# Encoder layer with window and neighbourhood attention: other times for the loads of keys and of the first gate, other places for buffers

## The chip, the cores and the metric

The kernel runs on one core of a Trainium2 chip. The metric is the device time of one execution in microseconds; "before" is the median of three runs. The engines are TensorE (PE in the profile, with its weight loads as PEld), VectorE (DVE), ScalarE (ACT), GpSimd (POOL) and SyncE (SP), which issues most DMAs. "SPq" is SP as a queue of DMA issues: it takes them strictly one after the other, and an issue that has to wait holds up all behind it.

## The reference

One layer of an encoder on 2048 tokens of width 1024, all in float32:

```python
z = rms_norm(x, norm_mix) @ w_in       # q_A k_A v_A q_B k_B v_B gate_A gate_B
yA = windowed_gqa(q_A, k_A, v_A, sink) # |t-s| <= 128, ALiBi, 8 heads, 2 of keys, one sink logit a head
yB = neighborhood_attn(q_B, k_B, v_B, rpb)  # 32 x 64 token grid, 8 x 16 neighbourhood, learned bias, 8 heads
x  = x + (sigmoid(gate_A) * (yA @ w_proj_a) + sigmoid(gate_B) * (yB @ w_proj_b)) @ w_out
x  = x + relu(rms_norm(x, norm_mlp) @ w_up) ** 2 @ w_down
out = rms_norm(x, norm_final)
```

## The kernel before, in words

Every large product is a sum of three matmuls (a high and a low part of each operand, lines 202 to 204 and 281 to 283), with float32 results in PSUM. The phases follow each other: norm and `w_in`, attention A, attention B, the end of the projections with `w_out`, up, down. Matrix work of another kind is put between the small matmuls of both attentions, so that PE has something to do while a softmax runs: in A the gates (`gate_tiles`), in B the last gates and then the projection of A's result (`proj_tiles`). `paced` deals this work out over the attention's units.

**Attention A** has 32 units. Its score is written by L858 and L859, its weights are turned by L893 and multiplied with the values by L878 and L879. L860 takes a unit's scores out of PSUM and adds a bias from `biasa0` or `biasa1`, one for each group of heads; the last units use `biasa1`. **Attention B** has 8 heads of 4 units (units 0 to 31, `attn_b`). A unit loads its queries (`qb`, L1094) and values (`vb`, L1097, a list `v_loads` keeps these loads), multiplies queries with the head's keys `kb` (L1107, four scores `s` of two matmuls), takes the scores out with a bias table added (L1112), exponentiates (L1118), scales them on GpSimd (L1123), turns the weights (L1153), splits them into `phb` and `plb` (L1159, L1160) and multiplies by the values (L1133). Keys of a head are 2 MB, in three DMAs (`load_k`, L1084 to L1086): the 128 rows, and the two halves of 64 rows with their places exchanged. Buffers `kb0` and `kb1` alternate with the head, so a head's load can start when the scores of the head before last are done. Bias tables (`biass` short, `biasl` long) are made by GpSimd (`make_bias_b`, L1075) from a raw table `braw` (L1061, L1063) and a mask.

**The projection** takes pairs of output columns f, f+1 for f = 0, 2, 4, 6. For each it loads and splits weights, and then for four pairs of (token blocks, column) loads a gate `z` of two halves (L996, 256 KB each), multiplies pages of y (`ypages`, the tiles `zh`) by the weights into the one PSUM buffer `mm`, and multiplies `mm` by the gate in place (L1013), which frees `mm`. The result goes out (`zp`, L175). One `z` is loaded ahead of the one in use.

**What sets the order.** The code emits instructions unit by unit, and a scheduler puts each engine's instructions into a row by its own estimates of when each can run; `tc.issue_after(x)` asks that a load be put behind instruction x. Pools are opened as two stacks in SBUF, from the left and from the right. Where B's pools lie on memory of A's, B's first load or write waits for A's last use of it. In before, `kb0` lies on `biasa1` and `ka0`, and so the keys of head 0 wait for the last unit of A to have used its bias.

Of the kernel before, what the change touches and what calls it, by code (L numbers as in the profile page):

```python
# [8 lines left out]
F32 = mybir.dt.float32  # L9
# [10 lines left out]
BH = 8  # L20
FF = 4096
EPS = 1e-6
P = 128
KC = D // P
NB = 4
BT = 512
# [23 lines left out]
def bias_layout():  # L50

    off, at = {}, 0
    start = []
    for j in (0, 1, 3):
        start.append(at)
        for i in (0, 1, 3):
            off[(JT[j], IT[i])] = at - start[-1]
            at += B_NR[i] * B_W[j]
        start.append(at)
    return off, start, at  # L60
# [32 lines left out]
def encoder_layer(ctx, tc, x, norm_mix, w_in, b_gate, sink, rpb, w_pa, w_pb, w_out,  # L93
                  norm_mlp, w_up, w_down, norm_final, dist_a, mask_b, out):
    nc = tc.nc
    V, A, G, PE, SY = nc.vector, nc.scalar, nc.gpsimd, nc.tensor, nc.sync

    def pool(name, side=None, space=None, stack=None):
        kw = {"reuse_waits": "tile"} if space is not DRAM else {}
        if side:  # L100
            kw["side"] = side
        if space:
            kw["space"] = space
        return (stack or ctx).enter_context(tc.tile_pool(name=name, bufs=1, **kw))

    def pools(stack, side, tags, name):

        return {t: pool(f"{name}_{t}", side=side, stack=stack) for t in tags}
# [9 lines left out]
    def psum(tag, bufs):  # L118
        n_ps[0] += 1
        return pps[tag].tile([P, 512], F32, tag=tag, bufs=bufs, name=f"{tag}_{n_ps[0]}")  # L120
# [3 lines left out]
    def T(pl, shape, dt, tag, bufs):  # L124
        n_t[0] += 1
        pl = pl[tag] if isinstance(pl, dict) else pl
        return pl.tile(shape, dt, tag=tag, bufs=bufs, name=f"{tag}_{n_t[0]}")
# [30 lines left out]
    zg = [[dp.tile([D, BT], F32, name=f"zg{b}{n}") for n in range(2)] for b in range(NB)]  # L158
# [11 lines left out]
    def put(dst, src):  # L170
        pending.append((dst, src))
# [5 lines left out]
    def split_weights(raw, hl, eng):  # L177
        A.copy(hl[:, 0], raw)
        eng.tensor_tensor(out=hl[:, 1], in0=raw, in1=hl[:, 0].bitcast(F32), op=ALU.subtract)
# [5 lines left out]
    def load_slice(parts):  # L185
        raw = T(wp, [P, KC, P], F32, "raw", 3)
        at = 0
        for ap, n in parts:
            SY.dma_start(raw[:, at : at + n, :], ap.rearrange("(k p) f -> p k f", p=P))
            at += n  # L190
        return raw

    def split_slice(raw, eng=G):
        hl = T(wp, [P, 2, KC, P], F32R, "whl", 2)
        split_weights(raw, hl, eng)
        return hl

    def cols(w, c, n=P):
        return w[:, c : c + n]

    def mm3(ps, lh, ll, rh, rl, first, last):
        PE.matmul(ps, lh, rh, start=first, stop=False)  # L202
        PE.matmul(ps, lh, rl, start=False, stop=False)  # L203
        PE.matmul(ps, ll, rh, start=False, stop=last)  # L204
# [373 lines left out]
    right = {n: (in_page[n](), in_page[n]()) for n in (1, 2)}  # L578
    tbanks = [(tpool, 2), (zpool[0], 1), (tpool, 2), (zpool[1], 1), (ypool[0], 1), (ypool[1], 1)]
    for k in range(KC):  # L580
        ps = zbank(*tbanks[k % 6])
        turned(ps, tiles[0], k)
        h, l = (t[:, k % 4] for t in right[1 + k // 4])
# [19 lines left out]
    for p in range(2):  # L603
        t = T(xp, [P, D], F32, "xin", 8).rearrange("p (k c) -> p k c", k=4)
# [15 lines left out]
    for k in range(KC):  # L620
# [8 lines left out]
        else:  # L629
            h, l = (t[:, kk] for t in right[3])  # L630
# [126 lines left out]
    for q in range(2, len(QUADS)):  # L757
# [5 lines left out]
        elif q in (6, 7):  # L763
            k = 2 * (q - 6)
# [8 lines left out]
        if q == SECOND:  # L773
            right, b0 = right2, 2
# [32 lines left out]
    wp = pools(s_w, "right", ("raw", "whl", "z"), "w")  # L807
    s_y = ExitStack()
    yb = T(pool("yb", side="left", stack=s_y), [P, BT], F32, "yb", 1)
    s_a = ExitStack()  # L810
    ap_ = pools(s_a, "left", ("dist", "sta", "qa", "ka1", "va1", "ya", "sa", "ph", "pl"), "a")
    ap_.update(pools(s_a, "right", ("biasa0", "va0", "ka0", "biasa1"), "a"))

    dist = T(ap_, [P, 384], F32, "dist", 1)
    SY.dma_start(dist, dist_a)
# [9 lines left out]
    ya = T(ap_, [P, BT], F32, "ya", 1)  # L825
# [158 lines left out]

    casts, now, v_loads = [], [0], []

    def proj_tiles(f):
        yield
        hl = split_slice(load_slice([(cols(w_pa[0], (f + i) * P), 4) for i in range(2)]), V)
        yield  # L990
        def load_z(b, i):
            z = T(wp, [P, 2, BT], F32, "z", 4)
            u = now[0] // 4 + 2
            with tc.issue_after(v_loads[u]) if u < len(v_loads) else nullcontext():
                for j in range(2):
                    SY.dma_start(z[:, j], zg[b + j][0][(f + i) * P : (f + i + 1) * P, :])  # L996
            return z

        z_next = load_z(0, 0)
        for b in (0, 2):  # L1000
            for i in range(2):
                z = z_next
                if b + i < 3:
                    z_next = load_z(*((b, 1) if i == 0 else (2, 0)))
                for j in range(2):
                    hi, lo = ypages[b + j]
                    ps = psum("mm", 1) if f + b < 8 else psum("s", 3)
                    for c in range(4):
                        cc = 4 * i + c
                        mm3(ps, hl[:, 0, cc, :], hl[:, 1, cc, :], hi[:, c], lo[:, c], c == 0, c == 3)  # L1010
                        if c == 1:
                            yield
                    V.scalar_tensor_tensor(out=z[:, j], in0=z[:, j], scalar=1.0, in1=ps, op0=ALU.add, op1=ALU.mult)  # L1013
                    put(zp[b + j][f + i], z[:, j])
                    yield

    fill = [gate_tiles(f) for f in range(14)] + [gate_tiles(14, 15)] + [proj_tiles(f) for f in range(0, 8, 2)]
    for n in (0, 0, 1):
        next(fill[n])
# [20 lines left out]


    s_b = ExitStack()
    bp = pools(s_b, "right", ("masks", "qb", "braw0", "biass", "stb", "kb0", "biasl", "braw1", "kb1"), "b")
    bp.update(pools(s_b, "left", ("sb0", "sb1", "vb0", "vb1", "sb2", "vb2", "phb", "plb"), "b"))
    boff, bstart, btotal = bias_layout()
    n_raw = [0]
    masks = T(bp, [P, btotal], mybir.dt.bfloat16, "masks", 1)
    with tc.issue_after(began[20]):
        SY.dma_start(masks, mask_b)
# [2 lines left out]
    def load_raw(h, jt):  # L1052
        j = (0, 1, 3)[jt]
        w = B_W[j]
        raw = T(bp, [P, 512], F32, f"braw{(n_raw[0] + 1) % 2 if n_raw[0] > 1 else 0}", 1)[:, : 16 * w]
        n_raw[0] += 1
        first = h * T_ROWS * w + (T_RO - 11) * w + (B_C0[j] - 16 * j - 15 + T_COFF[j])
        src = bass.AP(tabs[jt].tensor, tabs[jt].offset + first, [[w, 8], [1, 16], [1, 16 * w]])
        if n_raw[0] < 3:
            with tc.issue_after(began[20]):  # L1060
                SY.dma_start(raw, src)  # L1061
        else:
            G.dma_start(raw, src)  # L1063
        return raw

    def make_bias_b(raw, jt):
        j = (0, 1, 3)[jt]
        w = B_W[j]
        t = T(bp, [P, 40 * w], F32, "biasl" if jt == 1 else "biass", 1 if jt == 1 else 2)
        for i in (0, 1, 3):  # L1070
            n = B_NR[i] * w
            o = boff[(jt, IT[i])]
            at = (B_R0[i] - 8 * i + 4) * w
            out, mask, rows = t[:, o : o + n], masks[:, jstart[jt] + o : jstart[jt] + o + n], raw[:, at : at + n]
            G.tensor_tensor(out=out.rearrange("p (q x r) -> p q x r", x=w, r=4),  # L1075
                            in0=rows.rearrange("p (q r x) -> p q x r", x=w, r=4),
                            in1=mask.rearrange("p (q x r) -> p q x r", x=w, r=4), op=ALU.add)
        return t

    def load_k(h):  # L1080

        k = T(bp, [P, 2, S], F32R, f"kb{h % 2}", 1)
        kd = ks_b[h // 2][h % 2]
        SY.dma_start(k[:, 0].bitcast(F32), kd)  # L1084
        SY.dma_start(k[0:64, 1].bitcast(F32), kd[64:128])
        SY.dma_start(k[64:128, 1].bitcast(F32), kd[0:64])  # L1086
        return k

    def attn_b(n_u, h, j, k, bias):
        e, t = h % 2, h // 2  # L1090
# [74 lines left out]
    def all_b():  # L1165
        order = [(h, j) for h in range(BH) for j in ((0, 3, 1, 2) if h == 0 else range(4))]
        tables = [(h, JT[j]) for h, j in order if j != 2]
        raws = [load_raw(*tables.pop(0))]
        for h in range(BH):
            k = load_k(h)  # L1170

            for n, j in enumerate((0, 3, 1, 2) if h == 0 else range(4)):
                if j != 2:
                    if tables:
                        raws.append(load_raw(*tables.pop(0)))
                    bias = make_bias_b(raws.pop(0), JT[j])
                u = attn_b(4 * h + n, h, j, k, bias)
                next(u)
                yield u
# [8 lines left out]


    units = ahead_of(all_b(), 1)  # L1190
    drive((next(units) for _ in range(15)), live, False)
    given = [0]
# [446 lines left out]
    for m in range(2):  # L1639
# [31 lines left out]
        for f in range(8):  # L1671
            if m:
                i = f // 4
# [25 lines left out]
    for _ in range(2):  # L1699
        right = next(rights)  # L1700
# [7 lines left out]
    for m in range(2):  # L1708
        if m:
            right = next(rights)  # L1710
# [203 lines left out]
```

## Time and profile before

| | |
|---|---|
| median of 3 runs | 2612.0 us (2609.64 to 2612.59) |
| the profiled execution | 2609.07 us, span 2607.3 us |
| mean granted clock of TensorE | 0.996 |
| PE busy | 2545.3 us, 98% of the span |
| DVE, ACT, POOL busy | 1702.5, 1310.4, 410.1 us |
| DMA | 552.39 MB, mean 212 GB/s |
| scores of attention B | 783 to 1079 us |

In the profile's rows a bracket behind an instruction tells how long its engine stood idle before it, and what ended that. A row of a timeline has the start, the duration, the engine, the line, the operation, output and input tile. A row of the chain of waits has the start, the duration and what ran or was waited for. A window row gives length, busy time of PE, PEld, DVE, ACT and POOL (with counts of instructions), the granted clock, the busy share of the DMA engines, and GB/s.

### The profile page before, as it was taken

How to read it: one execution, taken by the hardware profiler on the slowest of the kernel's cores; microseconds unless marked ns; L12 is line 12 of the kernel's file. 1: busy time of each engine (PE TensorE's matmuls, PEld its weight loads, DVE VectorE, ACT ScalarE, POOL GpSimd, SP SyncE). 2: the span in 40 equal slices, each digit the busy share in tenths (PEclk: the TensorE clock that was granted, in tenths of full speed). 3: DMA queues.
4: the chain of work that ended last, by engine and by line, in shares of the span. 5: the costliest groups of instructions: out<-in, count | busy, mean ns of one | idle time of the engine just before them, and what ended most of it. 6: DMA issues, size and time to landing. Idle time of an engine off the chain costs nothing.

```text
span 2607.3 us, 34583 instructions
## 1 busy us (share of the span) xinstructions
PE 2545.3 (98%) x11936; PEld 2116.8 (81%) x11936; DVE 1702.5 (65%) x2693; ACT 1310.4 (50%) x2345; POOL 410.1 (16%) x506
## 2 busy tenths in 40 slices
PE   8999999999998989999999999999999999999998
PEld 6788888887877978888887888888887888888887
DVE  8857577666674566746588667766665635554766
ACT  6365464557775665514256555644444322323444
POOL 1001001133445755220312000000000000000011
PEclk9999999999999999999999999999999999999999
DMA  5768878774357899688888665844427825444555
GB/s 186 222 197 254 272 233 280 223 219 115 92 141 204 220 264 262 221 291 311 280 322 253 227 218 210 285 171 156 157 103 297 297 98 185 145 155 160 186 197 166
DMA packets 347999, 552.39 MB, mean 212 GB/s; under 512 B 32120, under 2 KB 152424, under 8 KB 345776
## 3 DMA queue, kind: packets, MB, share of 16 engines
q1 hardware_dynamic: 330640, 509.66, 61.2%
q10 hardware_dynamic: 10944, 24.12, 2.5%
q0 software_dynamic: 6240, 16.40, 2.1%
q8 instruction: 94, 1.54, 0.3%
q14 instruction: 81, 0.66, 0.1%
HBM read 363.35 MB, written 186.71 MB: 211 GB/s over the span
## 4 chain that ended last, share of the span: by engine, by line
PE 83%; DVE 6%; DMA 5%; ACT 2%; issue 2%; SPq 1%; POOL 1%; POOLq 0%; DVEq 0%; ACTq 0%
PE b L282 16%; PE b L283 16%; PE b L281 16%; PE zb L281 5%; PE zb L283 5%; PE zb L282 5%; PE mm L202 3%; PE mm L204 3%; PE mm L203 3%; PE av L1133 2%; PE pt L1153 2%; PE s L1107 1%; PE pt L893 1%; PE b L202 1%; PE b L203 1%
## 5 line engine op out<-in xcount | busy, mean ns | idle before, releaser
L282 PE MATMUL b<-dwh,dah 128*128 128x512 f32 x896 | 348.7, 389 | 0.4 <-DVE dwh L278 0.4
L283 PE MATMUL b<-dwh,dah 128*128 128x512 f32 x896 | 347.8, 389 | 0.0
L281 PE MATMUL b<-dwh,dah 128*128 128x512 f32 x896 | 338.0, 389 | 1.7 <-ACT dwh L277 1.7
L277 ACT CAST dah<-da 128x1024 fp32r<-128x1024 f32 (+1 forms) x128 | 120.9, 945 | 367.9 <-PE b L283 245.6
L281 PE MATMUL zb<-zh,zwhl 128*128 128x512 f32 x728 | 284.9, 392 | 3.8 <-ACT zc L488 1.4
L282 PE MATMUL zb<-zh,zwhl 128*128 128x512 f32 x728 | 285.0, 391 | 0.0
L278 DVE TENSOR_TENSOR dah<-da,dah 128x1024 fp32r<-128x1024 f32 (+1 forms) x128 | 139.1, 1089 | 222.7 <-ACT dah L277 222.6
L283 PE MATMUL zb<-zh,zwhl 128*128 128x512 f32 x728 | 283.5, 391 | 0.8 <-DVE zwhl L278 0.8
L281 PE MATMUL b<-ubh,uwhlb 128*128 128x512 f32 x592 | 230.2, 389 | 2.6 <-ACT uc L1488 1.6
L282 PE MATMUL b<-ubh,uwhlb 128*128 128x512 f32 x592 | 230.4, 389 | 1.1 <-DVE ubh L278 1.1
L283 PE MATMUL b<-ubh,uwhlb 128*128 128x512 f32 x592 | 229.0, 389 | 0.0
L281 PEld LDWEIGHTS b<-dwh,dah 128*128 128x128 f32 x896 | 168.1, 188 | 36.9 <-ACT dwh L277 2.1
L282 PEld LDWEIGHTS b<-dwh,dah 128*128 128x128 f32 x896 | 168.2, 188 | 35.7 <-DVE dwh L278 0.8
L283 PEld LDWEIGHTS b<-dwh,dah 128*128 128x128 f32 x896 | 168.2, 188 | 34.9
L272 DVE TENSOR_TENSOR uc<-b,uc 128x512 f32<-128x512 f32 x160 | 108.8, 688 | 113.6 <-PE b L283 107.7
L202 PE MATMUL mm<-zh,whl 128*128 128x512 f32 x368 | 155.5, 423 | 10.6 <-DVE z L1013 9.8
L281 PEld LDWEIGHTS zb<-zh,zwhl 128*128 128x128 f32 x728 | 136.9, 188 | 34.4 <-ACT zc L488 2.5
L283 PEld LDWEIGHTS zb<-zh,zwhl 128*128 128x128 f32 x728 | 136.9, 188 | 29.2 <-DVE zwhl L278 1.3
L282 PEld LDWEIGHTS zb<-zh,zwhl 128*128 128x128 f32 x728 | 137.0, 188 | 27.7
L204 PE MATMUL mm<-zh,whl 128*128 128x512 f32 x368 | 145.1, 394 | 0.0
L203 PE MATMUL mm<-zh,whl 128*128 128x512 f32 x368 | 144.8, 393 | 0.0
L281 PEld LDWEIGHTS b<-ubh,uwhlb 128*128 128x128 f32 x592 | 111.2, 188 | 26.3 <-ACT uc L1488 2.0
(268 smaller groups left out, 5730.8 us busy)
## 6 DMA issues: line engine op xcount, KB each, us to landing
at<-uc SPq DMA_DIRECT2D x224, 256.0 KB, 2.1
da<-at SPq DMA_DIRECT2D x96, 512.0 KB, 3.5
dw<-in_w_down_dram SPq DMA_DIRECT2D x160, 256.0 KB, 5.4
uraw<-in_w_up_dram SPq DMA_DIRECT2D x32, 1024.0 KB, 6.8
pgl<-wo_d SPq DMA_DIRECT2D x28, 1024.0 KB, 6.7
zraw<-in_w_in_dram SPq DMA_DIRECT2D x24, 1024.0 KB
z<-zg SPq DMA_DIRECT2D x64, 256.0 KB, 5.3
qs_a<-ze SPq DMA_DIRECT2D x32, 256.0 KB, 5.6
```

The costliest lines, as they stand in the source:

```text
L202: PE.matmul(ps, lh, rh, start=first, stop=False)
L203: PE.matmul(ps, lh, rl, start=False, stop=False)
L204: PE.matmul(ps, ll, rh, start=False, stop=last)
L272: return eng.tensor_tensor(out=out, in0=a, in1=b, op=op).ins
L277: rounded[0] = A.copy(hi, src).ins
L278: return eng.tensor_tensor(out=lo, in0=src, in1=hi.bitcast(F32), op=ALU.subtract).ins
L281: PE.matmul(ps, lh, rh, start=first, stop=False, skip_group_check=True)
L282: PE.matmul(ps, lh, rl, start=False, stop=False, skip_group_check=True)
L283: PE.matmul(ps, ll, rh, start=False, stop=last, skip_group_check=True)
L893: last = PE.transpose(pt[:, h * P : (h + 1) * P], s[:, h, c * P : (c + 1) * P], ident).ins
L1133: PE.matmul(po[0][:, i0 * P : (i0 + ni) * P], v[:kp, c, :], src[:kp, o : o + ni * P], start=first[0], stop=(c == 7 and z == 1), skip_group ...
L1153: last = PE.transpose(pt[:kp, at + (i - i0) * P : at + (i - i0 + 1) * P], s[i][:, rr : rr + kp], ident)
```

## The change

It has three parts. (1) `biasa1` goes from the right stack to the left, and B's pools on the right are put in another order, `kb0` directly after the masks; the two short bias tables get pools of their own. `kb0` then lies on keys and values of A's group 0, whose last use is in unit 20 of A's 32. `biass1`, the second short table's buffer, comes to lie where `biasa1` is. (2) `load_k` becomes a generator: the three loads of head h+1 are issued one by one at the second, third and fourth unit of head h, each behind the last load of values that the code has emitted; head 0's are issued together in front. (3) The first gate of the first pair (f = 0) is loaded right behind its weights, one step earlier and without `issue_after`; all others are as they were.

```diff
-    ap_ = pools(s_a, "left", ("dist", "sta", "qa", "ka1", "va1", "ya", "sa", "ph", "pl"), "a")
-    ap_.update(pools(s_a, "right", ("biasa0", "va0", "ka0", "biasa1"), "a"))
+    ap_ = pools(s_a, "left", ("dist", "sta", "qa", "ka1", "va1", "ya", "sa", "ph", "pl", "biasa1"), "a")
+    ap_.update(pools(s_a, "right", ("biasa0", "va0", "ka0"), "a"))
...
+    def load_z(f, b, i, tied=True):
+
+        z = T(wp, [P, 2, BT], F32, "z", 4)
+        u = now[0] // 4 + 2
+        with tc.issue_after(v_loads[u]) if tied and u < len(v_loads) else nullcontext():
+            for j in range(2):
+                SY.dma_start(z[:, j], zg[b + j][0][(f + i) * P : (f + i + 1) * P, :])
+        return z
+
     def proj_tiles(f):
         yield
         hl = split_slice(load_slice([(cols(w_pa[0], (f + i) * P), 4) for i in range(2)]), V)
-        yield
...
-        z_next = load_z(0, 0)
+        z_next = load_z(f, 0, 0, False) if f == 0 else None
+        yield
+        z_next = z_next or load_z(f, 0, 0)
...
-    bp = pools(s_b, "right", ("masks", "qb", "braw0", "biass", "stb", "kb0", "biasl", "braw1", "kb1"), "b")
+    bp = pools(s_b, "right", ("masks", "kb0", "qb", "braw0", "stb", "biass0", "biass1", "biasl", "braw1", "kb1"), "b")
...
-        t = T(bp, [P, 40 * w], F32, "biasl" if jt == 1 else "biass", 1 if jt == 1 else 2)
+        n_short[0] += jt != 1
+        t = T(bp, [P, 40 * w], F32, "biasl" if jt == 1 else f"biass{1 - n_short[0] % 2}", 1)
...
-        SY.dma_start(k[:, 0].bitcast(F32), kd)
-        SY.dma_start(k[0:64, 1].bitcast(F32), kd[64:128])
-        SY.dma_start(k[64:128, 1].bitcast(F32), kd[0:64])
-        return k
+        for to, src in ((k[:, 0], kd), (k[0:64, 1], kd[64:128]), (k[64:128, 1], kd[0:64])):
+            with tc.issue_after(v_loads[-1]) if v_loads else nullcontext():
+                SY.dma_start(to.bitcast(F32), src)
+            yield k
...
+        for k_next in load_k(0):
+            pass
         for h in range(BH):
-            k = load_k(h)
-
+            k = k_next
...
+                if n == 1 and h < BH - 1:
+                    pieces = load_k(h + 1)
+                if n and h < BH - 1:
+                    k_next = next(pieces)
```

The lines of `attn_b` move down by three (L1107 becomes L1110), the load of the gate is L993, and all three loads of keys are L1089. The rows below are the instructions of an engine in the order in which it takes them.

On SP, at the change of the attentions, before: the keys of head 0 (`ks_b0`), behind them stores of A's result and values of B.

```order
299 L1084 DMA kb0_809_7469<-ks_b0_88 128x2048
300 L1085 DMA kb0_809_7469<-ks_b0_88 64x2048
301 L1086 DMA kb0_809_7469<-ks_b0_88 64x2048
302 L175 DMA y_a1_143<-yb_482_4489 64x4x128
303 L1097 DMA vb1_825_7530<-vs_b0_92 96x4x256
304 L175 DMA y_a1_143<-ya_484_4531 64x4x128
```

And now, some 20 rows earlier, with the queries `qa` of A's last units behind them.

```order
280 L1089 DMA kb0_809_7472<-ks_b0_88 64x2048
281 L175 DMA y_a0_142<-ya_484_4531 64x4x128
282 L1089 DMA kb0_809_7472<-ks_b0_88 64x2048
283 L847 DMA qa_743_6705<-qs_a11_79 128x4x128
284 L175 DMA zg20_102<-z_797_7212 128x512
285 L1063 DMA braw0_810_7476<-tab2_154 128x1x384
```

On PE at the same place: the last scores of A (L858, L859) before, and what followed them.

```order
3233 L858 MATMUL s_6931<-ka_486_4533,qa_6915 128x256
3234 L859 MATMUL s_6931<-ka_486_4533,qa_6915 128x256
3235 L878 MATMUL av_6831<-ph_6839,va_488_4535 128x512
3236 L879 MATMUL av_6831<-pl_6840,va_488_4535 128x512
3237 L893 MATMUL pt_6892<-ident,sa_6707 128x128 x4
```

Now the first scores of B's unit 0 (`kb`, `qb`) stand there; they stood 35 rows further on.

```order
3233 L858 MATMUL s_6931<-ka_486_4533,qa_6915 128x256
3234 L859 MATMUL s_6931<-ka_486_4533,qa_6915 128x256
3235 L878 MATMUL av_6831<-ph_6839,va_488_4535 128x512
3236 L1110 MATMUL s_7497<-kb_809_7472,qb_7482 128x288 x2
3237 L1110 MATMUL s_7502<-kb_809_7472,qb_7482 128x384 x2
3238 L879 MATMUL av_6831<-pl_6840,va_488_4535 128x512
```

On SP, at the start of the projection's matmuls, before: behind a page of y (`zh2`) and the values of unit 16 stand the first and the second gate (two loads each).

```order
391 L979 DMA zh2_1377_10904<-y_a0_142 128x2x512
392 L979 DMA zh2_1377_10904<-y_a1_143 128x2x512
393 L1097 DMA vb1_1086_9201<-vs_b2_94 96x4x256
394 L996 DMA z_1380_10917<-zg00_98 128x512
395 L996 DMA z_1380_10917<-zg10_100 128x512
396 L1094 DMA qb_1135_9482<-qs_b2_86 128x4x128
397 L996 DMA z_1381_10920<-zg00_98 128x512
398 L996 DMA z_1381_10920<-zg10_100 128x512
```

Now a piece of head 5's keys (`kb1`) and the second gate stand there; the first gate is 45 rows ahead.

```order
349 L993 DMA z_1060_8995<-zg00_98 128x512
350 L993 DMA z_1060_8995<-zg10_100 128x512
351 L1100 DMA vb0_950_8225<-vs_b1_93 128x4x256
352 L1089 DMA kb1_933_8131<-ks_b1_89 64x2048
```

```order
391 L979 DMA zh2_1378_10911<-y_a1_143 128x2x512
392 L1100 DMA vb1_1088_9209<-vs_b2_94 96x4x256
393 L1089 DMA kb1_1086_9205<-ks_b2_90 64x2048
394 L993 DMA z_1381_10924<-zg00_98 128x512
395 L1097 DMA qb_1136_9488<-qs_b2_86 128x4x128
396 L993 DMA z_1381_10924<-zg10_100 128x512
```

The three pieces of head h + 1 stand in SP's row each right behind a load of values: of the last unit of head h − 1, and of the first and the second unit of head h.

More of the change, by code (lines that the diff above doesn't have):

```diff
@@ L989, in proj_tiles @@
         hl = split_slice(load_slice([(cols(w_pa[0], (f + i) * P), 4) for i in range(2)]), V)
+        z_next = load_z(f, 0, 0, False) if f == 0 else None
         yield
[L991 to L997, printed above, removed]
-        z_next = load_z(0, 0)
+        z_next = z_next or load_z(f, 0, 0)
         for b in (0, 2):
@@ L1003, in proj_tiles @@
                 if b + i < 3:
-                    z_next = load_z(*((b, 1) if i == 0 else (2, 0)))
+                    z_next = load_z(f, *((b, 1) if i == 0 else (2, 0)))
                 for j in range(2):
@@ L1042, in encoder_layer @@
     s_b = ExitStack()
-    bp = pools(s_b, "right", ("masks", "qb", "braw0", "biass", "stb", "kb0", "biasl", "braw1", "kb1"), "b")
+    bp = pools(s_b, "right", ("masks", "kb0", "qb", "braw0", "stb", "biass0", "biass1", "biasl", "braw1", "kb1"), "b")
     bp.update(pools(s_b, "left", ("sb0", "sb1", "vb0", "vb1", "sb2", "vb2", "phb", "plb"), "b"))
     boff, bstart, btotal = bias_layout()
-    n_raw = [0]
+    n_raw, n_short = [0], [0]
     masks = T(bp, [P, btotal], mybir.dt.bfloat16, "masks", 1)
```

## The prediction

> **What bounds the kernel now.** I read the page first, for the shares of the engines (busy us, share, instructions).
>
> ```profile
> PE 2545.3 (98%) x11936; PEld 2116.8 (81%) x11936; DVE 1702.5 (65%) x2693; ACT 1310.4 (50%) x2345; POOL 410.1 (16%) x506
> ```
>
> TensorE is busy for 2545.3 of 2607.3 us, and the change leaves its matmuls as they are. So only two things can be won: pieces of the 62 us in which PE stands still, and matmuls that run at a lowered clock. I asked for PE's waits in the stretch that the change touches, 760 to 1090 us: attention B with the output projection beside it (waiter, releaser, us in total, times, longest).
>
> ```profile
> PE mm L202 <- DVE z L1013: 9.8, 3, 6.9
> PE av L1133 <- DVE plb L1160: 3.5, 6, 0.8
> PE s L1107 <- DMA kb<-ks_b: 3.3, 2, 1.9
> PE s L1107 <- DVE stb L1112: 2.5, 4, 0.9
> ```
>
> The first row is the gate of the projection, the third the first head's keys; the change works on both. The other two belong to softmax, and nothing is taken from them. Then I followed the two rows through the timelines, down to the transfer that ends each.
>
> **Part (a), the keys of head 0.** Issues on SP, the scores that wait on PE, one row of GpSimd, and the stretch in which the load now runs as a window (length, busy us of PE, PEld, DVE, ACT and POOL, clock, DMA's busy share, GB/s).
>
> ```profile
> 718.39 0.34 SPq L1049 DMA_DIRECT2D masks<-in_mask_b_dram  x1
> 773.47 0.52 SPq L1084 DMA_DIRECT2D kb<-ks_b  x1
> 772.38 0.28 PE L859 MATMUL s<-ka,qa 128*128 128x256 f32 x1
> 783.21 0.76 PE L1107 MATMUL s<-kb,qb 128*128 128x288 f32 x3 [1.38 <-DMA kb<-ks_b]
> 786.97 0.73 PE L1107 MATMUL s<-kb,qb 128*128 128x288 f32 x3 [1.87 <-DMA kb<-ks_b]
> 777.11 1.84 POOL L871 TENSOR_SCALAR sa<-sa,sta 128x256 f32<-128x256 f32 x4 [7.09 <-ACT ph L897]
> 720.00:740.00 20.00, 19.76 (x102) 15.86 (x101) 15.20 (x36) 14.70 (x40) 13.27 (x16) 1.00 0.61 177
> ```
>
> Before, the keys are issued at 773.47 us, and both waits on them end in the 13.5 us behind that. After, their three loads stand right behind the masks, which were issued at 718.39, while the first scores move up to just behind A's last scores (772.38). Lead: about 54 us, against the 15.2 us that the slowest 1 MB load of keys in this trace took (the row stands below). So 1.38 + 1.87 = 3.25 us of waiting go. What they moved past: SP's loads of queries for A's last units, which have 2 MB more ahead of them; the DMA had room there (share 0.61, 177 GB/s), and I take 0. What is late next: unit 0's four evictions and exponentials now lie ahead of some of A's casts on VectorE and ScalarE, and PE may wait for a cast. The nearest rows are the waits on plb, 3.5 us over 6, so 0.6 each. I take one of them, 0.6; the bounds are none and five (3.0). The second short bias table has a new wait on GpSimd, for A's last use of the buffer that it lies on, the eviction behind A's last score (772.38); GpSimd stands idle there for 7.09 us until 777.11, and a table is three operations: 0. **(a) = −3.25 + 0.6 = −2.65**, from −3.25 to −0.25.
>
> **Part (b), the first gate.** SP's issue, the same transfer in the chain of waits, then VectorE and PE beside it; the windows are the stretch ahead of the stall and the one behind it.
>
> ```profile
> 944.24 2.52 SPq L996 DMA_DIRECT2D z<-zg  x2
> 944.24 12.40 DMA z<-zg
> 947.51 0.55 DVE L1160 TENSOR_TENSOR plb<-pt,phb 128x384 fp32r<-128x384 f32 x1
> 956.74 0.69 DVE L1013 SCALAR_TENSOR_TENSOR z<-z,mm 128x512 f32<-128x512 f32 x1 [8.68 <-DMA z<-zg]
> 957.49 0.79 PE L202 MATMUL mm<-zh,whl 128*128 128x512 f32 x1 [6.86 <-DVE z L1013]
> 968.98 0.67 DVE L1013 SCALAR_TENSOR_TENSOR z<-z,mm 128x512 f32<-128x512 f32 x1
> 940.00:950.00 10.00, 8.94 (x56) 7.76 (x56) 6.78 (x15) 7.72 (x19) 5.37 (x7) 1.00 1.08 264
> 957.50:961.00 3.50, 3.50 (x10) 2.92 (x11) 3.21 (x6) 0.00 (x0) 1.70 (x1) 0.53 1.09 351
> ```
>
> The load takes 12.40 us from its issue, VectorE stands for 8.68 and PE for 6.86 us. There is one PSUM buffer for this matmul, so PE can't go on until VectorE has multiplied by the gate. Behind the stall PE works for 3.5 us at a clock of 0.53, which does 1.86 us of work: 1.65 us more are lost. After, this load is issued with the weights, ahead of the values of 877.44 (the row stands below) and so about 70 us early: both go, 8.5 us in all.
>
> What is late next is the second gate, needed at the third of these multiplications. That stood at 968.98, 12.2 us behind the first; 10.6 at the full clock. VectorE was free for the first from 948.1, so the need comes at 958.7. The load is now issued where the first one was, with half a MB of keys ahead of it (some 1.9 us at 264 GB/s), so by the first one's 12.40 us it lands between 944.24 + 12.40 = 956.6, if the half MB costs nothing, and 945.5 + 12.4 + 1.9 = 959.8. In all, 0.5 MB of keys less has been issued ahead of it than ahead of the first one before, so I lean to the earlier end: a residual wait of 0 to 1.1, taken as 0.3. The chain behind it runs closer on VectorE and ScalarE without the pause: one more wait of 0.6. **(b) = −8.5 + 0.3 + 0.6 = −7.6**, from −8.5 to −6.
>
> This clock bears a rule. The half clock follows here also on short waits:
>
> ```profile
> 806.75 0.39 PE L879 MATMUL av<-pl,va 128*128 128x512 f32 x1
> 807.59 9.71 DMA braw<-tab
> 817.46 3.61 POOL L1075 TENSOR_TENSOR biasl<-braw,masks 128x384 f32<-128x384 f32 x3 [6.43 <-DMA braw<-tab]
> 817.50:821.00 3.50, 1.79 (x12) 1.27 (x11) 2.13 (x6) 1.27 (x2) 3.50 (x3) 0.98 1.01 233
> 821.00:824.30 3.30, 3.30 (x12) 2.86 (x13) 3.10 (x10) 1.82 (x6) 0.68 (x2) 0.50 1.06 261
> ```
>
> PE was idle for 1.7 of 3.5 us, and 3.3 us at 0.50 came behind it, again 1.65 us, so I price any new wait of that length with the clock's loss on top. The Trainium skill ("TensorE: Matmul & The Clock Gate", Part 1: The HAM clock gate) has the clock halved after at least one idle window of about 3.4 us; here 1.7 us of idle time sufficed, so the trace does not bear it out as a threshold. By that rule a new wait of 2 or 3 us at the second gate would leave the time at the wait alone, 1.65 us lower than the row makes it.
>
> **Part (d), the first long table.** That same stall stays. Its raw table lies where A's last pl was and is issued after A's last matmul (806.75) in both kernels, lands 9.71 us later, and the order has as much PE work between that matmul and the score that waits. I take 0, ±1.7 for the clock's phase.
>
> **Part (c), keys in pieces.** SP and PE, and between them rows of landing times (min/median/max from issue to landing: the gates in 975 to 980 us, the keys in 970 to 977, a page of y in 900 to 960, the values in 905 to 915).
>
> ```profile
> 974.37 1.98 SPq L1086 DMA_DIRECT2D kb<-ks_b  x1
> 978.49 1.22 SPq L996 DMA_DIRECT2D z<-zg  x2
> 996.54 0.50 PE L202 MATMUL mm<-zh,whl 128*128 128x512 f32 x1 [1.15 <-DVE z L1013]
> 1012.13 0.50 PE L202 MATMUL mm<-zh,whl 128*128 128x512 f32 x1 [1.75 <-DVE z L1013]
> DMA to landing us min/median/max: 17.2/17.2/17.2
> DMA to landing us min/median/max: 15.2/15.2/15.2
> DMA to landing us min/median/max: 12.7/12.7/12.7
> DMA to landing us min/median/max: 8.9/8.9/8.9
> 877.44 0.54 SPq L1097 DMA_DIRECT2D vb<-vs_b  x1
> 889.74 0.52 PE L1107 MATMUL s<-kb,qb 128*128 128x288 f32 x2
> 912.54 0.54 SPq L1097 DMA_DIRECT2D vb<-vs_b  x1
> 925.31 0.43 PE L1107 MATMUL s<-kb,qb 128*128 128x288 f32 x2
> 997.08 0.54 SPq L1097 DMA_DIRECT2D vb<-vs_b  x1
> 1009.14 0.43 PE L1107 MATMUL s<-kb,qb 128*128 128x288 f32 x2
> ```
>
> The gate issued at 978.49 had 2 MB of keys just ahead and took 17.2 us; it cost PE 1.15. After, 1 MB is ahead, some 3.8 us less: −1.15. The wait of 1.75 at 1012 had no keys near it and stays. Moving the pieces costs lead. The last one stands behind the values of a head's second unit, and the next head's first scores follow at 889.74 − 877.44 = 12.3, 12.8 and 12.1 us (heads 3, 4 and 6). By the values' 8.9 us it is in time by 3; with the 12.7 of the page of y it is 1.0, 0.5 and 1.2 late, 2.7 in all. Being 0.5 MB against the values' 0.5, I take 8.9 and its own 1.9 more, 10.8: no wait. **(c) = −1.15**, from −1.5 to +1.5. The piece stands behind a load of values that is issued after that unit's scores are done, so SP does not stand there. Where the order of the final down projection shifts a little, no matmul waits: 0, up to +1.
>
> **The sum.** −2.65 − 7.6 − 1.15 = −11.4. The profiled execution took 2609.07 us (span 2607.3 and 1.8 around it), 2.9 below the median of the three runs, 2612.0. From the execution it gives 2597.7, from the median 2600.6. I predict 2600.
>
> **Rivals.** *R1, the stall only moves:* the second gate, the y pages or a softmax wait take the place of the first gate, since DMA is full from 940 to 960 (shares over 1.0). With the first wait gone, the second gate landing by the later gate's 17.2 us at 945.5 + 17.2 = 962.7 instead of 958.7: 4 us of wait and the lowered clock's 1.65 come back. Then −11.4 + 5.65 = −5.75: 2606 from the median. For it: 17.2 us was measured under keys just ahead; against: half a MB, not two.
>
> *R2, slower: the last piece of keys comes late.* It decides above a landing of about 12 us. At 17.2 us, heads 3, 4 and 6 would wait 17.2 + 0.6 − 12.3 = 5.5, 5.0 and 5.7: 16.2 us, and three lowered clocks 5.0. Then −11.4 + 21.2 = +9.8: 2622; at 12.7 its 2.7 us leave it faster. For it: three leads of 12 us in a stretch of full DMA. Against: the pieces take the bursts away that made the 17.2.
>
> *R3, no change:* the gain at the change of attentions comes back at the long table, which PE reaches earlier, and (b) goes as in R1: −11.4 + 2.65 + 5.65 = −3.1, some 2609. Little speaks for it: the table's load is triggered by PE's own work and moves along.
>
> **Numbers.** Forecast 0.68, R1 0.16 (still faster), R3 0.08, R2 0.08. About 0.2% (5 us) can be told from no change. The forecast's and most of R1's cases are faster, a few of R1's and R3's fall within: faster 0.82, same 0.09, slower 0.09. The range: low −3.25 − 8.5 − 1.5 − 1.7 = −15 from the execution, 2594; high R1's and R3's edge, 2609.
>
> **Right or wrong in the new profile.** No wait of s on kb near 772 to 787; the first gate multiplied near 945 to 949 with no DMA before it, no clock below 1 between 945 and 961; the half clock near 820 still there; the wait at 996 gone, that at 1012 left. I am wrong if waits of scores on kb show at heads 3, 4 or 6, or if the wait on z at the third multiplication is over 2 us.

## The result, and the profile after

| | before | changed kernel |
|---|---|---|
| median | 2610.05 us (6 runs, 2606.70 to 2612.59) | 2600.51 us (6 runs, 2597.18 to 2601.92) |
| ratio | | 0.9959, 95% interval 0.9947 to 0.9971 |
| span of the profiled execution | 2607.3 us | 2599.3 us |
| half clock in the profile, past its first 40 us and before its last 20 | at 821, 954 (6.8 us), 1391 | at 924, 965, 1382 (6.8 us) |

A half clock lasts 3.4 us in these profiles, or a multiple of that. The changed kernel is faster by 9.5 us by the medians and by 10.7 by the ratio, against a forecast of 11.4 (2600 us, where 2600.5 was measured). PE's waits between 760 and 1090 us in the changed kernel (waiter, releaser, us in total, times, longest):

```profile
PE av L1136 <- DVE plb L1163: 4.5, 8, 1.0
PE s L1110 <- DVE stb L1115: 3.8, 3, 3.1
PE s L1110 <- DMA kb<-ks_b: 3.5, 1, 3.5
PE mm L202 <- DVE z L1015: 1.1, 1, 1.1
```

The 9.8 us on the gate are 1.1, and the two waits on head 0's keys are gone. But the row on `kb` has hardly changed its sum: it is another wait, 180 us later. Windows (columns as ahead of the prediction), the first of the kernel before, the others of the changed kernel; then the changed kernel's three longest waits of PE:

```profile
950.00:960.00 10.00, 3.14 (x13) 2.41 (x12) 3.26 (x7) 3.15 (x7) 0.70 (x1) 0.70 1.10 278
780.00:800.00 20.00, 20.00 (x109) 16.89 (x108) 10.17 (x24) 13.22 (x32) 13.59 (x17) 1.00 0.40 111
950.00:960.00 10.00, 9.53 (x63) 8.52 (x62) 9.72 (x19) 7.55 (x17) 5.82 (x5) 1.00 1.10 292
960.00:970.00 10.00, 6.53 (x31) 5.63 (x30) 4.33 (x12) 3.56 (x12) 6.67 (x10) 0.83 1.03 252
```

```profile
816.38 0.62 PE L1110 MATMUL s<-kb,qb 128*128 128x384 f32 x2 [3.06 <-DVE stb L1115]
965.24 0.51 PE L1110 MATMUL s<-kb,qb 128*128 128x288 f32 x1 [3.47 <-DMA kb<-ks_b]
1004.55 0.50 PE L202 MATMUL mm<-zh,whl 128*128 128x512 f32 x1 [1.11 <-DVE z L1015]
```

PE has no gap at all from 780 to 800, where 3.25 us were. From 950 to 960 it works for 9.53 us; before, the stall on the gate left 3.14 of the same ten. From 760 to 1090 PE stands still for 14.0 us in all, where it was 20.6. What is new is the wait at 965 for the last piece of head 5's keys, with a half clock behind it, and a longer one at the first long table (816). VectorE's first and third multiplication by a gate come without a wait for a DMA:

```profile
945.54 0.68 DVE L1015 SCALAR_TENSOR_TENSOR z<-z,mm 128x512 f32<-128x512 f32 x1
958.38 0.67 DVE L1015 SCALAR_TENSOR_TENSOR z<-z,mm 128x512 f32<-128x512 f32 x1
```

SP's row shows why the piece at 965 is late, and SP's waits (waiter, releaser, total, times, longest; 944 to 955 us) show what held it:

```profile
945.62 2.92 SPq L189 DMA_DIRECT2D raw<-in_w_proj_b_dram  x2
950.91 2.17 SPq L175 DMA_DIRECT2D y_b<-yb  x1
954.14 0.55 SPq L1100 DMA_DIRECT2D vb<-vs_b  x1
954.74 1.06 SPq L1089 DMA_DIRECT2D kb<-ks_b  x1
```

```profile
SPq L189 <- DMA zh<-y_a: 3.9, 2, 2.1
SPq L175 <- DMA vb<-vs_b: 2.3, 1, 2.3
```

SP stood for transfers to land before it issued the next. The trace tells which: the kernel's DMAs on SP take eight semaphores, here in turn, and each waits until the DMA with the same semaphore, eight issues before it, has landed. So no more than eight are in flight here. The first load of weights (L189, 945.62) waited for a page of y issued at 936.66, the values at 954.14 for the first half of the second gate, issued at 940.19, and the piece at 954.74 for queries issued at 942.12.

In the kernel before, the values of unit 17 and head 5's first scores stood here (of the four matmuls of the second row, the last two are head 5's, from 972.03):

```profile
958.32 0.54 SPq L1097 DMA_DIRECT2D vb<-vs_b  x1
971.76 0.69 PE L1107 MATMUL s<-kb,qb 128*128 128x288 f32 x4
```

The values, and with them the piece, were issued only 4.2 us earlier than before (954.14 against 958.32), while PE came to head 5's first score 10.6 us earlier (961.47 against 972.03). The lead fell from 13.7 to 7.3 us, and the piece needed 10.5 us from its issue to PE's release at 965.24.

### The profile page after: what moved, and what is told of

Same layout as the page of the kernel before. It is cut to its first block, busy times and chain, and to the rows that moved or that the text cites. A ratio compares the mean times of both kernels' runs of the same rounds, so it can differ in the third digit from the quotient of the medians.

```text
span 2599.3 us, 34574 instructions
## 1 busy us (share of the span) xinstructions
PE 2545.2 (98%) x11936; PEld 2118.1 (81%) x11936; DVE 1702.7 (66%) x2693; ACT 1310.8 (50%) x2345; POOL 410.9 (16%) x506
## 4 chain that ended last, share of the span: by engine, by line
PE 83%; DMA 7%; DVE 6%; ACT 3%; issue 2%; SPq 0%; POOL 0%; ACTq 0%; DVEq 0%; POOLq 0%
PE b L282 16%; PE b L283 16%; PE b L281 16%; PE zb L281 5%; PE zb L283 5%; PE zb L282 5%; PE mm L202 3%; PE mm L203 3%; PE mm L204 3%; PE av L1136 2%; PE pt L1156 1%; PE s L1110 1%; PE pt L893 1%; PE b L202 1%; PE b L203 1%
```

## The experiments

**Each part alone, and the change without the pieces.** These four ran on one chip, where before took 2611.12 us. The rows of a kernel come from one of its executions, whose time can lie some us from the median (2603.74 against 2607.91 in `pieces_only`).

```diff
 # gate_only: the kernel before, and
...
+        z_next = load_z(0, 0, False) if f == 0 else None
         yield
+        z_next = z_next or load_z(0, 0)
```

> The kernel before with part (3) alone: the first gate is loaded with its weights, keys and places stay. Theory (the stall and its half clock go, 8.5 us, and nothing of that size takes their place): 6.5 to 8.5 us below before, no wait of the projection over 2 us near 945 to 965. Rival (the stall only moves, to the second gate or the pages, since DMA is full there): 0 to 4 us below, with a new wait on z, zh or kb in its place.

Measured: 2602.65 us, ratio 0.9971 (0.9958 to 0.9984), 7.6 us below by the ratio. PE's waits:

```profile
PE mm L202 <- DVE z L1014: 3.9, 2, 2.4
PE s L1108 <- DMA kb<-ks_b: 3.9, 2, 2.2
```

The waits on `kb` are head 0's (at 786 and 790). No wait of the projection stands near 945 to 965; the later gates, at 992 and 1009, take 3.9 us, where they took 2.9 before. The theory holds: the largest part of the gain is this one load.

```diff
 # places_only: the kernel before, with the new pools and biass0, biass1; load_k and load_z as they were
```

> The kernel before with part (1) alone: other places for the buffers, so that head 0's keys can load early; gate and pieces stay as before. Theory: the waits of 3.25 us on the first keys go, the stall at the first long table grows by about 1.4 us and its half clock may go or stay with the place of the stall in the clock's windows (1.65 us): 2 to 3.5 us below before. Rival (the gain comes back whole at the long table): within 1 us of before.

Measured: 2605.51 us, ratio 0.9983 (0.9973 to 0.9994), 4.4 us below by the ratio. Three rows of its waits:

```profile
PE mm L202 <- DVE z L1013: 8.3, 4, 6.1
PE s L1108 <- DMA qb<-qs_b: 2.7, 1, 2.7
PE s L1108 <- DVE stb L1113: 1.6, 3, 0.8
```

The waits on head 0's keys are gone, and the stall at the long table did not grow here (0.8 at most). Other waits moved, though: a wait of 2.7 us on queries came at 827 (0.5 before), and those on gates and tables are 2.4 us less in all. The theory's −2 to −3.5 lies inside the interval, the rival's −1 outside.

```diff
 # pieces_only: the kernel before, with the new load_k and its calls
```

> The kernel before with part (2) alone: keys in pieces, first gate and places as before. Theory: the first gate's load has 0.5 to 1 MB less ahead of it, so its stall is 1 to 3 us shorter, and the later gate's wait of 1.15 us goes; with PE held by the first gate the last piece of head 5 is in time: 1 to 4 us below before. Rival (pieces come late at heads 4 to 6 by themselves): 1 to 6 us above before, with a wait of scores on kb.

Measured: 2607.91 us, ratio 0.9991 (0.9980 to 1.0003), 2.4 us below by the ratio, not clear of zero.

```profile
PE mm L202 <- DVE z L1013: 5.6, 2, 5.2
PE s L1107 <- DVE stb L1112: 3.8, 2, 3.4
```

The first gate's stall is 1.7 us shorter (5.2), as less lies ahead of it, and no piece is late at heads 4 to 6. But the stall at the long table is 3.4 us here, where the places alone have 0.8: that cost belongs to the pieces, not to the places.

```diff
 # no_pieces: the changed kernel, with load_k as before (three loads in one go at the head's start)
```

> The changed kernel without part (2): first gate early and other places, but each head's keys in one burst of 2 MB, as before. Theory: the changed kernel's wait of 3.5 us on the last piece of head 5 and the half clock behind it (1.65 us) go, and the waits of about 1 us that bursts cost the later gates come back: 2 to 4 us below the changed kernel, 11 to 14 below before. Rival (the pieces pay, since bursts hold the second gate up): 0 to 4 us above the changed kernel, 6 to 10 below before, with waits on z near 955 to 1000.

Measured: 2600.94 us, ratio 0.9961 (0.9947 to 0.9974). The changed kernel stood at 0.9959 in the first series: no difference that the intervals could tell. The medians do not bear out the theory, 2 to 4 us below it; the rival's 0 to 4 us above holds at its lower edge.

```profile
PE mm L202 <- DVE z L1014: 3.4, 2, 2.6
PE s L1109 <- DMA qb<-qs_b: 2.9, 1, 2.9
PE s L1109 <- DVE stb L1114: 1.6, 3, 0.8
```

The waits on pieces and table are gone, and bursts put others in their place: 2.6 and 0.8 on gates, 2.9 on queries. What the pieces take and give is about equal. The raw bias table shows how they take. In the changed kernel, SP's loads of head 1's keys and GpSimd's load and use of the raw table:

```profile
802.17 1.50 SPq L1089 DMA_DIRECT2D kb<-ks_b  x3
803.40 0.60 POOL L1065 DMA_DIRECT2D braw<-tab  x1 [4.61 <-PE pt L1156]
814.61 3.61 POOL L1078 TENSOR_TENSOR biasl<-braw,masks 128x384 f32<-128x384 f32 x3 [5.86 <-DMA braw<-tab]
```

And without pieces, where the other two loads of keys follow at 803.38 and 804.61:

```profile
802.76 0.57 SPq L1086 DMA_DIRECT2D kb<-ks_b  x1
802.54 0.60 POOL L1064 DMA_DIRECT2D braw<-tab  x1 [4.51 <-PE pt L1155]
811.45 3.65 POOL L1077 TENSOR_TENSOR biasl<-braw,masks 128x384 f32<-128x384 f32 x3 [3.57 <-DMA braw<-tab]
```

With the 2 MB ahead of it GpSimd has the table 11.2 us after its issue, with them behind it after 8.9. That is 2.3 us, as much as the stall differs (3.06 against 0.81).

**The clock, the late piece and the table.** Four kernels on another chip, where before took 2609.83 us. The first is the changed kernel once more.

```diff
 # again: the changed kernel, nothing edited
```

> The changed kernel once more, unchanged. Theory (a half clock comes when the waits of PE fall together in one window of a grid of 3.41 us that runs on its own, so where the grid lies decides which waits cost it): the same waits of PE to within a few tenths of a us, half clocks at other places or in another number than in the first profile, runs spread over 4 us or more. Rival (the half clock belongs to the place in the program): half clocks again at 924, 965 and 1382 us. Time: 8 to 10 us below before.

Measured: 2597.52 us, ratio 0.9947 (0.9931 to 0.9964). Its waits:

```profile
PE s L1110 <- DVE stb L1115: 3.9, 3, 3.2
PE s L1110 <- DMA kb<-ks_b: 1.3, 1, 1.3
```

The late piece costs 1.3 us here, where it cost 3.5: its size depends on the run, and the waits did not stay within a few tenths of a us as the theory had it. The runs spread over 3.3 us and not 4, and the time is 12.3 us below before by the medians, not 8 to 10. Half clocks lie at 544, 817 and 1377 us, so they moved as the theory had it, but for the last, near which the first profile had one too. The stall at the table is the same (3.19 against 3.06), and now a half clock follows. Windows around it in this profile, and after that in the first one of the same kernel, both along the clock's steps to within 0.2 us:

```profile
813.60:817.00 3.40, 0.85 (x5) 0.68 (x6) 1.09 (x4) 0.00 (x0) 2.62 (x3) 1.00 1.10 343
817.00:820.40 3.40, 3.40 (x16) 2.78 (x15) 3.40 (x11) 0.99 (x3) 1.62 (x2) 0.52 0.56 159
```

```profile
811.72:815.13 3.41, 1.60 (x8) 1.07 (x7) 0.00 (x0) 1.55 (x3) 0.52 (x1) 1.00 1.06 263
815.13:818.55 3.42, 2.10 (x13) 1.54 (x13) 2.41 (x8) 0.58 (x1) 3.09 (x3) 1.00 1.05 319
```

In the one run the stall falls into a single window (0.85 us busy) and the next is at half; in the other it is cut in two (1.60 and 2.10 busy) and costs no clock.

```diff
 # early_pieces: the changed kernel, and
-                    k_next = next(pieces)
+                    for _ in range((2, 1, 0)[n - 1]):
+                        k_next = next(pieces)
```

> The changed kernel with the two first pieces of a head's keys at the second unit and the last at the third: each head's last piece about one unit (9 us) earlier. Theory (the wait of 3.47 us at head 5 is the late last piece): no wait of scores on kb over 1 us; 2 to 5 us below the changed kernel. Rival (SP's queue is held by transfers in flight there, and what is issued earlier only pushes the second gate or the pages of y back): a wait of 2 to 4 us on z or zh near 950 to 970 in its place, and the same time as the changed kernel within 1.5 us.

Measured: 2596.98 us, ratio 0.9954 (0.9940 to 0.9968), 0.5 us under the changed kernel on the same chip: no difference. The wait on `kb` is gone, as the theory had it, and the time is the rival's. The longest wait lies not where the rival put it but at the second pair's first gate:

```profile
1004.67 0.79 PE L202 MATMUL mm<-zh,whl 128*128 128x512 f32 x1 [5.60 <-DVE z L1015]
```

The profiled execution took 2606.62 us, 9.6 above the median and the longest of the eleven. So this row shows what one execution lost; what took the place of the wait on `kb` in the others is not shown.

```diff
 # table_early: the changed kernel, and
-        raw = T(bp, [P, 512], F32, f"braw{(n_raw[0] + 1) % 2 if n_raw[0] > 1 else 0}", 1)[:, : 16 * w]
+        raw = T(bp, [P, 512], F32, f"braw{n_raw[0] % 2 if n_raw[0] > 2 else 0}", 1)[:, : 16 * w]
```

> The changed kernel with the third raw bias table (the first long one) in the other buffer, so that its load no longer waits for A's last matmul. Theory (the stall of 3.06 us at the first long table is its load of 11 us behind A's end, made longer by the 2 MB of keys of head 1 issued just ahead of it): that stall falls under 0.5 us, 2 to 4 us below the changed kernel. Rival (something else is late there too, as the queries of the next unit were where keys came in bursts): a wait on qb or kb of 2 to 3 us near 815 to 830 in its place, and within 1.5 us of the changed kernel.

Measured: 2594.63 us, ratio 0.9936 (0.9919 to 0.9953); 2.9 us below the changed kernel on this chip, though the intervals overlap. It has the lowest ratio of all kernels.

```profile
PE mm L202 <- DVE z L1015: 2.5, 1, 2.5
PE s L1110 <- DMA kb<-ks_b: 2.4, 2, 2.1
PE s L1110 <- DVE stb L1115: 0.8, 2, 0.4
```

The stall at the table is 0.4 us at most, and nothing took its place near 815 to 830: the table's load was its cause.

```diff
 # both_early: the edits of early_pieces and table_early together
```

> Both together, early pieces and early table. Theory: the gains add, 4 to 8 us below the changed kernel, about 2593 to 2596 where before takes 2610. Rival (waits only move): within 2 us of the changed kernel.

Measured: 2596.98 us, ratio 0.9945 (0.9926 to 0.9963). By the medians the gains do not add, and the rival was right. PE's longest wait, SP's row and SP's wait in it:

```profile
PE s L1110 <- DMA qb<-qs_b: 5.4, 1, 5.4
```

```profile
813.66 3.05 SPq L1089 DMA_DIRECT2D kb<-ks_b  x2
818.77 1.73 SPq L1097 DMA_DIRECT2D qb<-qs_b  x1
```

```profile
SPq L1089 <- PE s L1110: 2.4, 1, 2.4
```

The first piece of head 2 waits for head 0's last scores to free its buffer, two pieces are issued there, and the queries behind them are late.

**Around the best version.** Three more, on a chip where before took 2610.98 us.

```diff
 # table_gates: table_early, and
-        z_next = load_z(f, 0, 0, False) if f == 0 else None
+        z_next = load_z(f, 0, 0, False)
         yield
-        z_next = z_next or load_z(f, 0, 0)
```

> The early-table kernel, and the first gate of every pair loaded with its weights, not that of the first pair alone. Theory (the wait of 1 to 2.5 us near 994 to 1005 is the second pair's first gate, tied to a late load of values): that wait goes, 1 to 3 us below the early-table kernel, 0.992 to 0.993 of before. Rival (its load only pushes a page of y or the second gate back, or takes one of the four gate buffers too early): a new wait on z near 955 to 985, and 0 to 3 us above the early-table kernel.

Measured: 2601.90 us, ratio 0.9972 (0.9958 to 0.9985), above the early-table kernel by more than the intervals: the rival's sign, by a third way. The wait on z is gone. PE's waits, then SP's (1005 to 1024 us), then SP's row:

```profile
PE s L1109 <- DMA kb<-ks_b: 6.9, 2, 6.1
```

```profile
SPq L993 <- DMA zp<-z: 7.0, 1, 7.0
```

```profile
1021.27 0.80 SPq L993 DMA_DIRECT2D z<-zg  x2
1023.24 0.69 SPq L1088 DMA_DIRECT2D kb<-ks_b  x1
```

The early gate holds one of four buffers, so another gate's load waits on SP until a stored result has landed. For 7.0 us nothing passes, and the last piece behind it is late by 6.1. The profiled execution is the shortest of the twelve (2597.06 us), so these rows need not be all that the median lost.

```diff
 # table_act: table_early, and
-                SY.dma_start(to.bitcast(F32), src)
+                (A if h else SY).dma_start(to.bitcast(F32), src)
```

> The early-table kernel with the keys of heads 1 to 7 issued by ScalarE's queue and not by SP's. Theory (the last piece of head 5 is late because SP issues it some 4 us late, held behind transfers in flight): the wait on kb of 2.1 us goes and SP's other loads are on time, 1 to 3 us below the early-table kernel. Rival (the transfers themselves are slow where DMA is full, and an issue on ScalarE that waits for a free key buffer holds up exponentials and casts): waits on kb stay, new waits on phb or plb, 2 us or more above the early-table kernel.

Measured: 2600.02 us, ratio 0.9959 (0.9942 to 0.9976). Both half right: there is no wait at head 5 any more, and no new one on the casts (plb 3.2 us in all), but others at 818 and 834. The time is on the rival's side, 6 us above the early-table kernel by the ratios, though the intervals overlap.

```profile
PE s L1110 <- DMA kb<-ks_b: 2.9, 1, 2.9
PE s L1110 <- DMA qb<-qs_b: 2.3, 1, 2.3
```

The wait on `kb` is head 1's now, whose load ScalarE issued at 802.70 where SP issued it at 799.20.

```diff
 # table_nopieces: no_pieces, with the edit of table_early
```

> The early-table kernel with keys in bursts, that is without part (2) of the change. Theory (the pieces give about as much at the gates as they cost at head 5, so they are worth nothing): within 1.5 us of the early-table kernel, 0.993 to 0.995 of before, waits on z and qb in place of the one on kb. Rival (with the table out of the way the pieces pay): 2 us or more above the early-table kernel.

Measured: 2599.72 us, ratio 0.9958 (0.9941 to 0.9975), against 0.9936 with pieces: the rival's side, but the intervals overlap, so that the pieces pay here is likely and not shown.

```profile
PE s L1109 <- DMA kb<-ks_b: 5.7, 2, 5.4
PE mm L202 <- DVE z L1014: 2.1, 1, 2.1
```

## Why the prediction was right, and where it was off

**(a), −2.65 forecast.** The two waits went, 3.25 us, and PE had no gap from 780 to 800 us, where the 0.6 for a late cast was expected. The part alone gave 4.4 (1.6 to 7.1). That the new wait of the short table costs nothing agrees. One reading was wrong: the 15.2 us, told as those of a 1 MB load of keys and of the stretch from 970 to 977, belong to a load of half a MB issued at 1010.73. Nothing hangs on it against a lead of 54 us.

**(b), −7.6 forecast.** The part alone gave 7.6 (4.2 to 11). The second gate came in time, its two halves at 953.5 and 955.3, for the third multiplication at 958.4; R1 did not happen. That the step had put the need at 958.7 is partly chance: the first multiplication came 2.6 us earlier than it said, and the third 12.8 us behind that and not 10.6. The half clock behind the stall went, as forecast. But this profile has others at 924 and 965, so that from 760 to 1090 the half clock costs about what it cost before, 3.4 us in both (an estimate: half of PE's busy time in those windows).

**(c), −1.15 forecast.** The waits of 1.15 and 1.75 became one of 1.11, a gain of 1.8. The step that failed is "no wait" for the last pieces. It measured leads as they stood in the profile before, and found them short at heads 3, 4 and 6. Those came in time, and so the signs named for being wrong did not show. Head 5, with the longest lead of the four (13.7 us), lost it: the prediction held that "SP does not stand there", but SP stood for the DMAs eight issues before and could not follow PE, which parts (a) and (b) had set free. The landing itself was sized well, 10.5 us against 10.8. So R2's late piece came at one head, at 3.5 us in one profile and 1.3 in the other, but not by R2's slow landing of over 12 us: the lead had shrunk. With the table's 2.3 us the pieces gave nothing on top of the other two parts (0.9959 with, 0.9961 without).

**(d), 0 ± 1.7 forecast.** The stall at the long table was said to stay as it was. It grew from 1.7 to 3.1 us, for the pieces put head 1's keys ahead of the table. The half clock behind it, said to stay, was absent in one profile and there in the other, as the bound of 1.7 allows.

**The casts, 0.6 in (a) and 0.6 in (b).** The waits on plb rose from 3.5 us in 6 to 4.5 in 8, so 1.0 of the 1.2 came, though none of it where (a) looked for it.

**The total** is right because (a) and (b), the large terms, are right and the misses are small. In the profile the late piece (3.5) and the table (1.4) cost 4.9 us; against them stand 0.6 at the gate of 1012, 0.3 that the second gate did not need, and 0.2 of casts. That 2600 was met to half a us is luck: the profiled executions differ by 8.0 us, the medians by 9.5, and the forecast was taken from a median of before of 2612.0, which stood at 2610.05 over six runs. The ratios of the three parts alone add up to 14.4 us; the whole gives 10.7 by its ratio in the first series and 13.8 in the second, each with 3 to 4 us to either side.

## What to carry to other kernels

When a stall on one queue is removed, recompute the leads of everything that is issued on that queue: a lead read from the old profile holds only if the issue moves with the consumer, and an issue that waits for earlier transfers to land does not. Count, too, how many DMAs the program lets be in flight on the queue (eight here). The first gate could be loaded 75 us earlier (869.19 against 944.24), and that alone gave 7.6 us; but a load that has to wait for a free buffer (the first piece of head 2's keys in `both_early`, a gate in `table_gates`) stops all that stands behind it on an in-order queue. Differences of 2 us in one profile need a second profile of the same kernel before they mean anything.

## What the runs showed of the hardware

The half clock is not a property of the place alone. Between 1373 and 1391 us one starts in ten of the 13 profiles and none in three; at the stall of the long table one profile of the changed kernel has it and the other does not. In the changed kernel's first profile half clocks start at 924.35 and 965.31 us, 40.96 apart, which is 12 steps of 3.413 us, and each lasts one step. The Trainium skill ("TensorE: Matmul & The Clock Gate", Part 1: The HAM clock gate) states a free-running window of 3413 ns. The trace agrees. The Trainium skill (same section) has the clock halved after at least one idle window. The traces do not bear that out: along these steps, in the 13 profiles, past their first 40 us and before their last 20, each of the 35 changes to the half clock followed a window in which PE was busy for 0.56 of the time or less. Every window at the full clock with less than 0.44 was followed by one, and between the two it went either way. Where the steps lie against the program differs from run to run, so about the same stall at the long table (3.0 to 3.2 us) came with no half clock in the changed kernel's first profile, with one step of it in the second, and with two in that of `early_pieces`; a step in which PE is busy costs some 1.65 us. That fits the spread of runs of one kernel (2602.88 to 2617.08 us for 31 runs of before), though how much of the spread it makes was not measured.
